# An encoder trunk in fp32: where the last sums of seven-product pairs are split, the order of the down pieces, the place of the norm's bias, and when the pooling bands are loaded

## The chip, the core and the metric

One of the eight cores of a Trainium2 chip runs the whole program. The metric is the device time of one execution in microseconds (us): a median over runs, and for single traces the span from the first to the last instruction. The engines have separate instruction queues, each worked through in its own order: PE multiplies matrices (weights are loaded by its second queue, PEld), DVE and ACT work on vectors, POOL does a little, SP issues the DMA transfers. A wait is a semaphore between two of them.

## The reference

Two post-norm layers over 256 tokens of width 2048, batch 1, all in fp32:

```
x <- LN(alpha*x + mixer(x));  x <- LN(alpha*x + SwiGLU(x))
def swiglu(x, w_gate, w_up, w_down):
    return (jax.nn.silu(x @ w_gate) * (x @ w_up)) @ w_down
def layer_norm(x, g, b):
    mu = jnp.mean(xf, axis=-1, keepdims=True)
    var = jnp.mean(jnp.square(xf - mu), axis=-1, keepdims=True)
    return ((xf - mu) * lax.rsqrt(var + LN_EPS)).astype(x.dtype) * g + b
```

Layer 0's mixer is neighbourhood attention beside a gated recurrence, layer 1's is a multi-scale pooling mixer beside grouped-query attention; each has an input and an output projection. The feed-forward width is 5632.

## The kernel before

**Splitting.** Each fp32 operand is held as a sum hi + lo of two rounded fp32r tensors, and a product takes three matmuls (`mm3`: lo x hi, hi x hi, hi x lo). `split` writes hi with an ACT cast (L122) and lo with a DVE subtraction (L123). The two token tiles of 128 rows are `tok` 0 and 1.

**Weights.** `load_half` brings a 512 KB piece (256 rows by 512 columns) into a buffer `raw` (four of them, in a ring), and splits it into `whi` and `wlo`; in the feed-forward units these have four buffers too, so a cast of `whi` waits until PE is done with the piece four before it.

**The feed-forward part.** The 5632 hidden columns are eleven chunks of 512. `whole` computes chunks 0 and 1 with plain products. The other nine are `unit`s 2 to 10. A unit computes gate and up products of its chunk for both token tiles together. For five of its eight row pairs (`SEVEN`, pairs 3 to 7) it uses a scheme of seven products in place of eight: `load_seven` loads 1 MB (`rs`), forms sums of weight blocks in `z`, and splits them into `sh` and `sl` (two buffers each). The first half of a unit runs four of the seven products for each of the five pairs (12 matmuls into the four banks `un`); between the halves some sums of the banks are formed (L488 to L493); the second half runs the other three products per pair in the order `ORDER` (3, 0, 4, 5, 1, 6, 7, 2), with plain pairs 0, 1, 2 between. One of the three, into bank c21, takes the last sum of the pair, the fourth slice of `z`. `load_seven` splits that sum too, in the first half: for the first three pairs into `zh`/`zl` (three buffers), for the last two into the room of `y4h`/`y4l`. All of `load_seven` is issued 400 places ahead of its place in the program, so the first two loads of a unit are worked on in the unit before.

**Down pieces.** The down projection of finished chunks is spread over the units by the generator `down_steps`: a round of two units (`ROUNDS`) works through the 16 pieces of two chunks: for each of four column quarters n, chunk by chunk, two pieces each; one `yield` (a step) per piece, 12 matmuls into two banks `acc`. With `run(1)` a unit runs three steps at its start, steps four to six between its first loads, and two more after the fifth load. Between steps 1, 2 and 3 stand the two `flips`: PE transposes the gated products of the previous unit, and ACT and DVE split them into that chunk's `yTh` and `yTl`. When a column quarter's last piece is done, both its banks are copied to `res` by ACT (L551), or in the first two quarters of the first round added to `res` by DVE (L549); ACT seeds a bank with `res` (L535). Unit 10 has a round of its own, with one chunk.

**Norms.** `norm` takes a token tile's statistics, subtracts the mean and multiplies by gamma on DVE (`centre`, L334), then scales by rstd on ACT (L348). `flip`, run in the middle of the next matmul chunk, transposes 512 columns at a time and adds the bias beta there, per partition from `betT`, in four ACT and four DVE instructions of 128 columns (L377, L379); `res` itself gets its beta by a DVE add (L381, L383). After the output projections that add is deferred by way of `idle_work`. There are three inner norms; the last one, which writes the output, has a branch of its own.

**Bands.** `cd_constants` loads what layer 1's mixer needs, and the banded matrices of the pooling (`band`, 1 MB, by way of two `raw` buffers), after the first of five input chunks.

The order of instructions on each engine is fixed when the program is built, by a scheduler that weighs priorities and a timing model; a row that ends `_3802` below names a tile by its number.

Of the kernel before, what the change touches and what calls it, by code (L numbers as in the profile page):

```python
# [78 lines left out]
def trunk(ctx: ExitStack, tc: tile.TileContext, a, out):  # L79
# [64 lines left out]

    idle_work = []

    def load_half(src, between=()):
# [38 lines left out]
    def mm_chunk(halves, lhs, outs, tok_major=False, after=None, before=None, seeded=False):  # L186
# [19 lines left out]
        if tok_major:  # L206
            for i, half in enumerate(halves):
                src = half[0]
                if pending and i >= FREE:
                    held[0] = 1  # L210
                loaded.append(load_half(src))
            for tok in range(NT):
                for i in range(n):
                    if pending and i >= FIRST_STEP:
                        step()
                    mms(i, tok, True)
                    if pending and tok == 0:
                        held[0] = HELD
                while pending:
                    step()  # L220
                if after:
                    after(tok)
        else:
            for i, half in enumerate(halves):
                src = half[0]
                loaded.append(load_half(src, before(i) if before else ()))
                if i >= n // 2:
                    with tc.issue_after(low[-1]):
                        for work in idle_work[:2]:
                            work()  # L230
                    del idle_work[:2]
# [74 lines left out]

    def residual_tools(res, gam, bet, betT, stats, defer=False):

# [14 lines left out]
        def norm(tok, xT=None, out_rows=None, late={}):  # L323
# [19 lines left out]
            if out_rows is None:  # L343
                for j in range(4):
                    dve = centre(j)
                for j in range(4):
                    r = cols(j)[0]
                    act = nc.scalar.activation(r, r, AF.Copy, scale=rstd[:, 0:1])  # L348
                ahead[:] = [dve.ins, act.ins]
                pending.append(flip(tok, xT))  # L350
            else:
                for j in (3, 0, 1):
                    tc.keep_in_program_order(centre(j))
                r, _, b = cols(3)
                nc.scalar.activation(r, r, AF.Copy, scale=rstd[:, 0:1])
                nc.gpsimd.tensor_tensor(r, r, b, op=add)
                for j in (0, 1, 2):
                    if j == 2:
                        tc.keep_in_program_order(centre(j))
                    tc.keep_in_program_order(scale(j))  # L360
                    store(j)
                store(3)

        def flip(tok, xT):
            for j in range(4):
                s = slice(j * NCH, (j + 1) * NCH)
                r = res[tok][:, s]
                with tc.high_priority(offset=1000):
                    t = mxp() if j % 2 else trp()
                    for k in range(4):  # L370
                        tc.keep_in_program_order(transpose(t[:, k * P : (k + 1) * P], r[:, k * P : (k + 1) * P], ident))
                    for part in range(2):
                        for k in range(4):
                            hi, lo = xT[0][tok][:, 4 * j + k, :], xT[1][tok][:, 4 * j + k, :]
                            tk, bk = t[:, k * P : (k + 1) * P], betT[:, 4 * j + k : 4 * j + k + 1]
                            if part == 0:
                                act = nc.scalar.activation(hi, tk, AF.Identity, bias=bk)  # L377
                            else:
                                dve = nc.vector.scalar_tensor_tensor(lo, tk, bk, hi.bitcast(F32), op0=add, op1=sub)  # L379
# [10 lines left out]
    def load_gb(pool, i, which):  # L390
# [3 lines left out]
        nc.sync.dma_start(b, a[f"ln_{which}_b"][i : i + 1, :].to_broadcast([P, D]))  # L394
        bT = pool.tile([P, 64], F32, tag="betT", name="betT", bufs=1)[:, :KT]
        nc.sync.dma_start(bT, a[f"ln_{which}_bT"][i])
        return g, b, bT


    def out_proj(w, order, groups, res, gb):  # L400
        seed, evac, norm = residual_tools(res, *gb, new_stats(), True)
        lhs = y_lhs(groups)
# [42 lines left out]
    def load_seven(sp, src, room):  # L445

        with tc.high_priority(offset=400):
            raw = sp.tile([P, 4, NCH], F32, tag="rs", name="rs", bufs=2)
            hi = sp.tile([P, 4, NCH], F32R, tag="sh", name="sh", bufs=2)
            lo = sp.tile([P, 4, NCH], F32R, tag="sl", name="sl", bufs=2)  # L450
            zh, zl = room or (sp.tile([P, NCH], F32R, tag=n, name=n, bufs=3) for n in ("zh", "zl"))
            z = sp.tile([P, 4, NCH], F32, tag="z", name="z", bufs=1)
            last_load[0] = nc.sync.dma_start(raw, src).ins
            nc.scalar.copy(hi[:, 0], raw[:, 0])  # L454
            nc.vector.tensor_tensor(z[:, :2], raw[:, 0:3:2], raw[:, 3:4].to_broadcast([P, 2, NCH]), op=add)
            nc.vector.tensor_tensor(z[:, 2], z[:, 0], raw[:, 2], op=add)  # L456
# [4 lines left out]
        return lambda i: (hi[:, i, :], lo[:, i, :]), (zh, zl)  # L461

# [3 lines left out]
    def unit(sp, w, lhs, forms, y, down, flips):  # L466
# [57 lines left out]
    def down_steps(w, chunks, ys, res, start):  # L524


        lhs = y_lhs(ys)
        for n in range(4):
            outs = [acc() for _ in range(NT)]
            r = [res[tok][:, n * NCH : (n + 1) * NCH] for tok in range(NT)]  # L530
            fresh = start and n < 2
            if not fresh:
                with tc.high_priority(offset=400):
                    for tok in range(NT):
                        nc.scalar.activation(outs[tok], r[tok], AF.Copy, scale=ALPHA if start else 1.0)  # L535
            steps = [(c, ci, i) for ci, c in enumerate(chunks) for i in range(2)]
            for c, ci, i in steps:
                hi, lo = load_half(w[n, 2 * c + i])
                for tok in range(NT):
                    for kk in range(2):  # L540
                        begin = (c, i, kk) == (chunks[0], 0, 0)
                        end = (c, i, kk) == (chunks[-1], 1, 1)
                        x = lhs(tok, 4 * ci + 2 * i + kk)
                        mm3(outs[tok], x, (hi[:, kk, :], lo[:, kk, :]), fresh and begin, end, True, skip_group_check=not fresh)
                half_done()
                if (c, i) == (chunks[-1], 1):
                    for tok in range(NT):
                        if fresh:
                            nc.vector.scalar_tensor_tensor(r[tok], r[tok], ALPHA, outs[tok], op0=mult, op1=add)  # L549
                        else:  # L550
                            nc.scalar.copy(r[tok], outs[tok])  # L551
                yield

    def ffn(layer, xT, res, mix_pool, close_mix, keep, last):
# [72 lines left out]
        stats = new_stats()  # L627
        seed, evac, _ = residual_tools(res, None, None, None, stats)
        yl = y_lhs([groups[c] for c in LAST])
# [325 lines left out]
    def cd_constants(pool):  # L955
# [11 lines left out]
        rcount = pool.tile([P, 4, 2, EDGE], F32, name="rcount", bufs=1)  # L967
        nc.sync.dma_start(rcount, a["rcount"])
        band = pool.tile([P, 4, NT, T], F32R, name="band", bufs=1)
        for g in range(0, 4, 2):  # L970
# [3 lines left out]
            nc.scalar.copy(band[:, s], raw)  # L974
        return cc, sn, nw, pscale, rcount, band

    def cd_mixer(mp, consts, xT, yT):
# [102 lines left out]
        for c, (kind, _) in enumerate(cd_plan()):  # L1080
            outs = [acc() for _ in range(NT)]
            mm_chunk([(a["cd_in"][c, n], two(2 * n)) for n in range(8)], lhs, outs, tok_major=(c == 0))
            if c == 0:
                with tc.issue_after(last_load[0]):
                    cc, sn, nw, pscale, rcount, band = cd_constants(consts.pop())
            if kind == "kv":
# [117 lines left out]
def layout(i):  # L1204
# [22 lines left out]
        "ln_ffn_b": f["ln_ffn_b"],  # L1227
        "ln_mix_bT": f["ln_mix_b"].reshape(2, KT, P).transpose(0, 2, 1),
        "ln_ffn_bT": f["ln_ffn_b"].reshape(2, KT, P).transpose(0, 2, 1),
    }  # L1230
# [26 lines left out]
```

## Time and profile before

| | us |
|---|---|
| median of 3 runs | 2205.69 (2205.14 to 2206.42) |
| the profiled execution | 2206.51 |
| its span | 2204.4 |
| PE busy | 2155.6 |
| DVE busy | 1704.3 |
| ACT busy | 1223.4 |
| idle time of PE ended by waits that the trace names | 37.9 |

The span is what the trace covers; the execution's own time is 2.1 us longer. The mean granted clock of PE over the span is 0.996. Matmuls of 512 columns start 0.227 us apart in steady work, so 12 of them take 2.72 us.

### The profile page before, as it was taken

How to read it: one execution, taken by the hardware profiler on the slowest of the kernel's cores; microseconds unless marked ns; L12 is line 12 of the kernel's file. 1: busy time of each engine (PE TensorE's matmuls, PEld its weight loads, DVE VectorE, ACT ScalarE, POOL GpSimd, SP SyncE). 2: the span in 40 equal slices, each digit the busy share in tenths (PEclk: the TensorE clock that was granted, in tenths of full speed). 3: DMA queues.
4: the chain of work that ended last, by engine and by line, in shares of the span. 5: the costliest groups of instructions: out<-in, count | busy, mean ns of one | idle time of the engine just before them, and what ended most of it. 6: DMA issues, size and time to landing. Idle time of an engine off the chain costs nothing. (4 is left out here: it accounts for less than half of the span.)

```text
span 2204.4 us, 27147 instructions
## 1 busy us (share of the span) xinstructions
PE 2155.6 (98%) x9910; PEld 1780.2 (81%) x9910; DVE 1704.3 (77%) x2194; ACT 1223.4 (55%) x1652; POOL 36.8 (2%) x43
## 2 busy tenths in 40 slices
PE   9999999999989999999999999999999999999998
PEld 7888888888878787887887788888787887888876
DVE  6886688667688888888886875666988888888866
ACT  6445544546455665665565654454555666566653
POOL 0000000000000000000000000000000000000000
PEclk9999999999999999999999999999999999999999
DMA  8555535674666776666665653655766666676744
GB/s 293 165 163 172 173 125 190 216 271 143 211 212 226 242 245 238 236 232 223 235 229 192 236 200 120 214 173 184 259 235 239 243 229 224 231 248 239 243 168 172
DMA packets 119190, 467.86 MB, mean 212 GB/s; under 512 B 14480, under 2 KB 17552, under 8 KB 106256
## 3 DMA queue, kind: packets, MB, share of 16 engines
q1 hardware_dynamic: 119056, 466.12, 61.7%
q8 instruction: 78, 1.28, 0.2%
q14 instruction: 56, 0.46, 0.1%
HBM read 463.97 MB, written 2.10 MB: 211 GB/s over the span
## 5 line engine op out<-in xcount | busy, mean ns | idle before, releaser
L123 DVE TENSOR_TENSOR wlo<-raw,whi 128x1024 fp32r<-128x1024 f32 (+1 forms) x671 | 815.9, 1223 | 319.1 <-ACT whi L122 312.6
L122 ACT CAST whi<-raw 128x1024 fp32r<-128x1024 f32 (+1 forms) x671 | 701.9, 1050 | 626.2 <-PE acc L296 338.6
L296 PE MATMUL acc<-whi,yTl 128*128 128x512 f32 x832 | 330.4, 397 | 13.1 <-DVE yTl L123 12.9
L296 PE MATMUL acc<-whi,yTh 128*128 128x512 f32 x832 | 325.4, 391 | 0.0
L296 PE MATMUL acc<-wlo,yTh 128*128 128x512 f32 x832 | 324.7, 391 | 0.0
L296 PE MATMUL acc<-whi,xTl 128*128 128x512 f32 x800 | 318.6, 398 | 4.9 <-ACT whi L122 4.9
L296 PE MATMUL acc<-whi,xTh 128*128 128x512 f32 x800 | 315.3, 394 | 0.0
L296 PE MATMUL acc<-wlo,xTh 128*128 128x512 f32 x800 | 313.2, 394 | 0.0
L296 PE MATMUL un<-whi,xTl 128*128 128x512 f32 x522 | 203.2, 389 | 0.0
L296 PE MATMUL un<-whi,xTh 128*128 128x512 f32 x522 | 203.1, 389 | 0.0
L296 PE MATMUL un<-wlo,xTh 128*128 128x512 f32 x522 | 203.1, 389 | 0.0
L296 PEld LDWEIGHTS acc<-whi,yTl 128*128 128x128 f32 x832 | 157.1, 189 | 48.5 <-DVE yTl L123 16.5
L296 PEld LDWEIGHTS acc<-wlo,yTh 128*128 128x128 f32 x832 | 156.9, 189 | 33.4
L296 PEld LDWEIGHTS acc<-whi,yTh 128*128 128x128 f32 x832 | 157.3, 189 | 31.3
L296 PEld LDWEIGHTS acc<-whi,xTl 128*128 128x128 f32 x800 | 151.3, 189 | 35.1 <-ACT whi L122 6.1
L296 PEld LDWEIGHTS acc<-wlo,xTh 128*128 128x128 f32 x800 | 151.1, 189 | 31.1 <-DVE wlo L123 0.6
L296 PEld LDWEIGHTS acc<-whi,xTh 128*128 128x128 f32 x800 | 151.4, 189 | 28.7
L123 DVE TENSOR_TENSOR sl<-z,sh 128x1536 fp32r<-128x1536 f32 x90 | 157.9, 1754 | 19.4 <-ACT sh L122 19.3
L122 ACT CAST sh<-z 128x1536 fp32r<-128x1536 f32 x90 | 133.0, 1478 | 16.8 <-DVE z L456 16.7
L454 ACT CAST sh<-rs 128x512 fp32r<-128x512 f32 x90 | 56.1, 624 | 149.5 <-DMA rs<-in_gu 64.7
L296 PEld LDWEIGHTS un<-wlo,xTh 128*128 128x128 f32 x522 | 98.0, 188 | 20.5
L296 PEld LDWEIGHTS un<-whi,xTh 128*128 128x128 f32 x522 | 98.0, 188 | 20.5
(279 smaller groups left out, 3093.1 us busy)
## 6 DMA issues: line engine op xcount, KB each, us to landing
raw<-in_gu SPq DMA_DIRECT2D x262, 512.0 KB, 4.4
rs<-in_gu SPq DMA_DIRECT2D x90, 1024.0 KB, 6.7
raw<-in_down SPq DMA_DIRECT2D x176, 512.0 KB, 4.4
raw<-in_ab_in SPq DMA_DIRECT2D x127, 512.0 KB, 4.2
raw<-in_cd_in SPq DMA_DIRECT2D x40, 512.0 KB, 4.2
raw<-in_ab_out SPq DMA_DIRECT2D x32, 512.0 KB, 4.5
raw<-in_cd_out SPq DMA_DIRECT2D x32, 512.0 KB, 4.3
bias<-in_na_bias SPq DMA_DIRECT2D x32, 64.0 KB, 4.0
```

The costliest lines, as they stand in the source:

```text
L122: nc.scalar.copy(hi, src)
L123: return nc.vector.tensor_tensor(lo, src, hi.bitcast(F32), op=sub).ins
L296: ins = nc.tensor.matmul(o, lhs[a], rhs[b], start=start and n == 0, stop=stop and n == 2, **more)
L454: nc.scalar.copy(hi[:, 0], raw[:, 0])
```

## The change

- `load_seven` no longer splits the last sum. It writes it as fp32 (`ze`) into a tile of its own for the first pair and into the rooms of `y4h` (pairs 4 and 5) and `y4l` (pairs 6 and 7) for the rest. `unit` splits it where the second half uses it, into two buffers `zfh`/`zfl`, with a priority of 400.
- `down_steps` takes two column quarters at a time and goes through both for the first chunk before it takes the second chunk. All four banks `acc` are in use at once, and a quarter is evacuated after the sixth and the eighth step of eight, no longer after the fourth and the eighth. The round of one chunk keeps its order.
- `norm` adds beta on DVE to the rows before they are transposed; `flip` is then one ACT cast and one DVE subtraction of 512 columns. `betT`, its loads and `idle_work` are gone.
- The bands are loaded after the second input chunk.

```
 def load_seven(sp, src, room):
-            zh, zl = room or (sp.tile([P, NCH], F32R, tag=n, name=n, bufs=3) for n in ("zh", "zl"))
-            z = sp.tile([P, 4, NCH], F32, tag="z", name="z", bufs=1)
+            z = sp.tile([P, 3, NCH], F32, tag="z", name="z", bufs=1)
+            ze = room
...
-            nc.vector.tensor_tensor(z[:, 3], z[:, 2], raw[:, 1], op=add)
+            nc.vector.tensor_tensor(ze, z[:, 2], raw[:, 1], op=add)
             nc.vector.tensor_tensor(lo[:, 0], raw[:, 0], hi[:, 0].bitcast(F32), op=sub)
-            split(hi[:, 1:], lo[:, 1:], z[:, :3])
-            split(zh, zl, z[:, 3])
+            split(hi[:, 1:], lo[:, 1:], z)
 def unit(sp, w, lhs, forms, y, down, flips):
-            if i == 3:
-                room = [x.rearrange("p (e a) t -> p e (a t)", e=2) for x in fourth()]
-            wt, edge[p] = load_seven(sp, w[p], room and [x[:, i - 3] for x in room])
+            if i % 2:
+                room = ap_.tile([P, 4, T], F32R, tag=("y4h", "y4l")[i // 2], name="ze4", bufs=1)
+                room = room.rearrange("p (e a) t -> p e (a t)", e=2).bitcast(F32)
+            own = room[:, (i + 1) % 2] if i else sp.tile([P, NCH], F32, tag="ze", name="ze", bufs=1)
+            wt, edge[p] = load_seven(sp, w[p], own)
...
-                product("c21", forms[p]["22"], edge[p])
+                with tc.high_priority(offset=400):
+                    ends = split_tile(sp, [P, NCH], edge[p], "zf", 2)
+                product("c21", forms[p]["22"], ends)
 def down_steps(w, chunks, ys, res, start):
-        for n in range(4):
-            outs = [acc() for _ in range(NT)]
-            fresh = start and n < 2
+        step = len(chunks)
+        for first in range(0, 4, step):
+            ns = range(first, first + step)
+            outs = {n: [acc() for _ in range(NT)] for n in ns}
+            fresh = start and first == 0
...
-            steps = [(c, ci, i) for ci, c in enumerate(chunks) for i in range(2)]
-            for c, ci, i in steps:
-                hi, lo = load_half(w[n, 2 * c + i])
+            for ci, c in enumerate(chunks):
+                for n in ns:
+                    for i in range(2):
+                        hi, lo = load_half(w[n, 2 * c + i])
 def norm(tok, xT=None, out_rows=None, late={}):
                 for j in range(4):
-                    dve = centre(j)
+                    centre(j)
                 for j in range(4):
-                    r = cols(j)[0]
+                    r, _, b = cols(j)
                     act = nc.scalar.activation(r, r, AF.Copy, scale=rstd[:, 0:1])
+                    dve = nc.vector.tensor_tensor(r, r, b, op=add)
 def flip(tok, xT):
-                    for part in range(2):
-                        for k in range(4):
-                            hi, lo = xT[0][tok][:, 4 * j + k, :], xT[1][tok][:, 4 * j + k, :]
-                            tk, bk = t[:, k * P : (k + 1) * P], betT[:, 4 * j + k : 4 * j + k + 1]
-                            if part == 0:
-                                act = nc.scalar.activation(hi, tk, AF.Identity, bias=bk)
-                            else:
-                                dve = nc.vector.scalar_tensor_tensor(lo, tk, bk, hi.bitcast(F32), op0=add, op1=sub)
-                if defer:
-                    idle_work.append(lambda r=r, s=s: nc.vector.tensor_tensor(r, r, bet[:, s], op=add))
-                else:
-                    nc.vector.tensor_tensor(r, r, bet[:, s], op=add)
+                    hi, lo = (x[tok][:, 4 * j : 4 * j + 4, :] for x in xT)
+                    v = t.rearrange("p (k t) -> p k t", k=4)
+                    act = nc.scalar.copy(hi, v)
+                    dve = nc.vector.tensor_tensor(lo, v, hi.bitcast(F32), op=sub)
 def cd_mixer(mp, consts, xT, yT):
+            if c == 1:
+                with tc.issue_after(last_load[0]):
+                    band = cd_bands(consts.pop())
```

The order of instructions at three places. First ACT around the fourth and fifth load of unit 6 of layer 0, before (`sh<-rs` is the cast of a load's first slice, `sh<-z` that of its three sums, `L488` the start of the sums between the halves):

```order
L122 CAST y4h<-z 128x512
L454 CAST sh<-rs 128x512
L122 CAST whi<-raw 128x1024
L122 CAST sh<-z 128x1536
L454 CAST sh<-rs 128x512
L122 CAST y4h<-z 128x512
L488 COPY g_7525<-un 128x512
```

and in the changed program at the same place:

```order
L437 CAST sh<-rs 128x512
L541 COPY res_3802<-acc 128x512
L524 ACTIVATE acc<-res_3802 128x512
L122 CAST whi<-raw 128x1024
L541 COPY res_3803<-acc 128x512
L122 CAST sh<-z 128x1536
L524 ACTIVATE acc<-res_3803 128x512
```

The casts of `y4h` are gone from here; the two copies of a column quarter and the seeds of the next, which stood some ten rows earlier, now stand between the fifth load's casts.

Second, DVE at the same place, before (`y4l` is the low part of a last sum; `L457` forms it):

```order
L123 TENSOR_TENSOR wlo<-raw,whi 128x1024
L123 TENSOR_TENSOR y4l<-z,y4h 128x512
L458 TENSOR_TENSOR sl<-rs,sh 128x512
L455 TENSOR_TENSOR z<-rs 128x1024
L456 TENSOR_TENSOR z<-z,rs 128x512
L123 TENSOR_TENSOR wlo<-raw,whi 128x1024
L457 TENSOR_TENSOR z<-z,rs 128x512
L123 TENSOR_TENSOR sl<-z,sh 128x1536
```

and changed:

```order
L123 TENSOR_TENSOR wlo<-raw,whi 128x1024
L438 TENSOR_TENSOR z<-rs 128x1024
L441 TENSOR_TENSOR sl<-rs,sh 128x512
L439 TENSOR_TENSOR z<-z,rs 128x512
L123 TENSOR_TENSOR wlo<-raw,whi 128x1024
L440 TENSOR_TENSOR ze_7431<-z,rs 128x512
L123 TENSOR_TENSOR sl<-z,sh 128x1536
```

The low part is gone; the last four rows keep their order, with the last sum going to `ze`.

Third, DVE near the start of unit 2 of layer 0, the first of its round, where the flips of chunk 1 are split (`yTl`), before:

```order
L123 TENSOR_TENSOR zl<-z,zh 128x512
L123 TENSOR_TENSOR wlo<-raw,whi 128x1024
L455 TENSOR_TENSOR z<-rs 128x1024
L123 TENSOR_TENSOR yTl<-un,yTh 128x4x128
L456 TENSOR_TENSOR z<-z,rs 128x512
L123 TENSOR_TENSOR wlo<-raw,whi 128x1024
L123 TENSOR_TENSOR yTl<-un,yTh 128x4x128
```

and changed:

```order
L123 TENSOR_TENSOR zfl<-ze_5280,zfh 128x512
L438 TENSOR_TENSOR z<-rs 128x1024
L439 TENSOR_TENSOR z<-z,rs 128x512
L123 TENSOR_TENSOR wlo<-raw,whi 128x1024
L440 TENSOR_TENSOR ze_5280<-z,rs 128x512
L123 TENSOR_TENSOR yTl<-un,yTh 128x4x128
L123 TENSOR_TENSOR wlo<-raw,whi 128x1024
L123 TENSOR_TENSOR yTl<-un,yTh 128x4x128
```

The sums of the third load now stand ahead of the first `yTl`. PE's own order has the same shapes in the same places; steps 3 and 4 of a round read other columns of the first chunk there in place of the second chunk.

More of the change, by code (lines that the diff above doesn't have):

```diff
@@ L143, in trunk @@
     first = [True]
-    idle_work = []
     def load_half(src, between=()):
@@ L226, in mm_chunk @@
                 loaded.append(load_half(src, before(i) if before else ()))
[L227 to L231, printed above, removed]
                 for kks in ((0,), (1,)) if before and i == 0 else ((0, 1),):
@@ L305, in new_stats, with residual_tools @@
         return [sm.tile([P, 4, 6], F32, tag=f"st{t}", name=f"st{t}", bufs=1) for t in range(NT)]
-    def residual_tools(res, gam, bet, betT, stats, defer=False):
+    def residual_tools(res, gam, bet, stats):
         def seed(tok, n, psum, scale):
@@ L394, in load_gb @@
         nc.sync.dma_start(b, a[f"ln_{which}_b"][i : i + 1, :].to_broadcast([P, D]))
-        bT = pool.tile([P, 64], F32, tag="betT", name="betT", bufs=1)[:, :KT]
-        nc.sync.dma_start(bT, a[f"ln_{which}_bT"][i])
-        return g, b, bT
+        return g, b
     def out_proj(w, order, groups, res, gb):
-        seed, evac, norm = residual_tools(res, *gb, new_stats(), True)
+        seed, evac, norm = residual_tools(res, *gb, new_stats())
         lhs = y_lhs(groups)
@@ L456, in load_seven @@
             nc.vector.tensor_tensor(z[:, 2], z[:, 0], raw[:, 2], op=add)
[L457 removed]
+            nc.vector.tensor_tensor(ze, z[:, 2], raw[:, 1], op=add)
             nc.vector.tensor_tensor(lo[:, 0], raw[:, 0], hi[:, 0].bitcast(F32), op=sub)
[L459 to L461 removed]
+            split(hi[:, 1:], lo[:, 1:], z)
+        return lambda i: (hi[:, i, :], lo[:, i, :]), ze
     BEGIN = ((0, "11", "c11"), (3, "f", "c12"), (1, "e", "c22"), (2, "g", "c21"))
@@ L527, in down_steps @@
         lhs = y_lhs(ys)
-        for n in range(4):
-            outs = [acc() for _ in range(NT)]
-            r = [res[tok][:, n * NCH : (n + 1) * NCH] for tok in range(NT)]
-            fresh = start and n < 2
+        step = len(chunks)
+        for first in range(0, 4, step):
+            ns = range(first, first + step)
+            outs = {n: [acc() for _ in range(NT)] for n in ns}
+            r = {n: [res[tok][:, n * NCH : (n + 1) * NCH] for tok in range(NT)] for n in ns}
+            fresh = start and first == 0
@@ L532, in down_steps @@
             if not fresh:
                 with tc.high_priority(offset=400):
-                    for tok in range(NT):
-                        nc.scalar.activation(outs[tok], r[tok], AF.Copy, scale=ALPHA if start else 1.0)
-            steps = [(c, ci, i) for ci, c in enumerate(chunks) for i in range(2)]
-            for c, ci, i in steps:
-                hi, lo = load_half(w[n, 2 * c + i])
[L539 to L552, printed above, removed]
+                    for n in ns:
+                        for tok in range(NT):
+                            nc.scalar.activation(outs[n][tok], r[n][tok], AF.Copy, scale=ALPHA if start else 1.0)
@@ new lines, in down_steps @@
+            for ci, c in enumerate(chunks):
+                for n in ns:
+                    for i in range(2):
+                        hi, lo = load_half(w[n, 2 * c + i])
+                        for tok in range(NT):
+                            for kk in range(2):
+                                begin = (ci, i, kk) == (0, 0, 0)
+                                end = (ci, i, kk) == (step - 1, 1, 1)
+                                x = lhs(tok, 4 * ci + 2 * i + kk)
+                                mm3(outs[n][tok], x, (hi[:, kk, :], lo[:, kk, :]), fresh and begin, end, True, skip_group_check=not fresh)
+                        half_done()
+                        if (ci, i) == (step - 1, 1):
+                            for tok in range(NT):
+                                if fresh:
+                                    nc.vector.scalar_tensor_tensor(r[n][tok], r[n][tok], ALPHA, outs[n][tok], op0=mult, op1=add)
+                                else:
+                                    nc.scalar.copy(r[n][tok], outs[n][tok])
+                        yield
@@ L627, in ffn @@
         stats = new_stats()
-        seed, evac, _ = residual_tools(res, None, None, None, stats)
+        seed, evac, _ = residual_tools(res, None, None, stats)
         yl = y_lhs([groups[c] for c in LAST])
@@ L968, in cd_constants, with cd_bands @@
         nc.sync.dma_start(rcount, a["rcount"])
+        return cc, sn, nw, pscale, rcount
+    def cd_bands(pool):
         band = pool.tile([P, 4, NT, T], F32R, name="band", bufs=1)
@@ L974, in cd_constants @@
             nc.scalar.copy(band[:, s], raw)
-        return cc, sn, nw, pscale, rcount, band
+        return band
     def cd_mixer(mp, consts, xT, yT):
@@ L1084, in cd_mixer @@
                 with tc.issue_after(last_load[0]):
-                    cc, sn, nw, pscale, rcount, band = cd_constants(consts.pop())
+                    cc, sn, nw, pscale, rcount = cd_constants(consts[0])
+            if c == 1:
+                with tc.issue_after(last_load[0]):
+                    band = cd_bands(consts.pop())
             if kind == "kv":
@@ L1227, in layout @@
         "ln_ffn_b": f["ln_ffn_b"],
-        "ln_mix_bT": f["ln_mix_b"].reshape(2, KT, P).transpose(0, 2, 1),
-        "ln_ffn_bT": f["ln_ffn_b"].reshape(2, KT, P).transpose(0, 2, 1),
     }
```

## The prediction

> **What bounds the kernel now.** I read the page's busy shares first, then the waits of PE alone, then the timeline around each of those waits.
>
> ```profile
> PE 2155.6 (98%) x9910; PEld 1780.2 (81%) x9910; DVE 1704.3 (77%) x2194; ACT 1223.4 (55%) x1652; POOL 36.8 (2%) x43
> ```
> ```profile
> PE acc L296 <- DVE yTl L123: 12.9, 9, 4.2
> PE un L296 <- DVE sl L123: 11.9, 18, 1.1
> PE acc L296 <- ACT whi L122: 4.9, 1, 4.9
> PE un L296 <- ACT sh L122: 2.4, 2, 1.2
> PE tr L119 <- ACT res L348: 2.2, 1, 2.2
> PE tr L119 <- DVE g L520: 1.9, 2, 1.1
> PE un L296 <- ACT un L492: 1.0, 2, 0.8
> PE un L119 <- DVE g L578: 0.7, 1, 0.7
> ```
>
> (In the second view: who waited for whom, us in total, times, longest.) PE is busy 98% of the span, and the change leaves it the same matmuls in streams of the same length. So only PE's waits can be won: 37.9 us in all, of which the 4.9 stand at the program's start, before the first weights, and the 1.9 at the two ends of the feed-forward layers, where nothing is changed. The rest, 31.1 us, is what the change can touch. Waits also cost speed behind them:
>
> ```profile
> 613.50:618.40 4.90, 4.85 (x11) 3.81 (x12) 3.62 (x5) 0.62 (x1) 0.00 (x0) 0.50 0.57 206
> 641.50:645.70 4.20, 4.16 (x11) 3.32 (x12) 4.17 (x7) 1.33 (x2) 0.00 (x0) 0.60 0.35 142
> 1572.00:1574.00 2.00, 1.66 (x6) 1.05 (x6) 2.00 (x3) 0.00 (x0) 0.00 (x0) 1.00 0.71 244
> ```
>
> (Columns: stretch, length, busy time of PE, PEld, DVE, ACT, POOL, then granted clock.) Behind the 4.24 us wait that ends at 613.55 the clock is 0.50 for 4.90 us, which loses 4.90 x 0.50 = 2.4 us; behind the two of about 1.1 us near 641 it is 0.60 for 4.2 us, 1.7 us; behind layer 1's counterpart of the first, which ends at 1572, it is 1.00.
>
> **Down pieces by chunk.** A round's first unit runs three down steps, with the previous unit's two flips between them. Now step 3 already takes the second chunk, whose transposes were issued just before:
>
> ```profile
> 877.25 0.58 ACT L122 CAST yTh<-un 128x512 fp32r<-128x512 f32 x1
> 877.38 1.22 DVE L123 TENSOR_TENSOR wlo<-raw,whi 128x1024 fp32r<-128x1024 f32 x1 [1.37 <-ACT whi L122]
> 878.52 0.68 DVE L123 TENSOR_TENSOR yTl<-un,yTh 128x512 fp32r<-128x512 f32 x1
> 879.26 0.50 PE L296 MATMUL acc<-whi,yTl 128*128 128x512 f32 x1 [0.94 <-DVE yTl L123]
> ```
>
> ```profile
> 1968.19 2.72 PE acc L296 x12
> ```
>
> After the change steps 1 to 4 all read the first chunk, and the second is first read in step 5. Between the second flip and step 5 PE has four groups of 12 matmuls (step 3, a load's first products, step 4, the next load's), 4 x 2.72 = 10.9 us by the row of the chain above; today yTl stands 2.9 us after that flip. These waits go whole. Rounds 2 to 4 have one of 0.94 each in both layers: 6 x 0.94 = **-5.6 us**. Nothing is late next there: the whi and wlo of steps 3 and 4 stand in the queues ahead of the flips' splits, as before.
>
> Round 1 has the larger ones, and there DVE is itself behind:
>
> ```profile
> 612.81 0.68 DVE L123 TENSOR_TENSOR yTl<-un,yTh 128x512 fp32r<-128x512 f32 x1
> 613.55 0.80 PE L296 MATMUL acc<-whi,yTl 128*128 128x512 f32 x1 [4.24 <-DVE yTl L123]
> 639.73 1.76 DVE L123 TENSOR_TENSOR sl<-z,sh 128x1536 fp32r<-128x1536 f32 x1 [0.51 <-ACT sh L122]
> 641.54 0.50 PE L296 MATMUL un<-sl,fnh 128*128 128x512 f32 x1 [1.06 <-DVE sl L123]
> ```
> ```profile
> L535 ACT ACTIVATE acc<-res 128x512 f32<-128x512 f32 x72 | 43.5, 604 | 3.7 <-DVE res L549 2.6
> ```
>
> (The last row groups ACT's seeds of a bank: count, busy time, mean ns.) In layer 0 the first unit loses 0.66 + 4.24 + 2.4 (clock) + 1.18 + 1.06 = 9.5 us up to the split of its fifth load. Afterwards: the new DVE order has one more sum (0.6) ahead of the first gated product, so the flip waits 1.2 in place of 0.66; the yTl wait is gone; and the evacuation of columns 0 now stands between the fifth load's sums. From the end of step 6 ACT has whi (1.05), a seed (0.60) and sh (1.48) to do before that split (1.76): 4.9 us, with DVE's evacuation (0.68, as yTl, of the same shape), wlo (1.22) and ze (0.68) beside them. PE asks for the split 17 matmuls after step 6, 17 x 2.72/12 = 3.85 us. So a wait of 1.0 is left at best, and 2.24 as today if DVE comes as late. I take 1.8 here, where the wait of 4.24 shows how late DVE is, and 1.0 in layer 1, where it is less late. Layer 0: 9.5 - 1.2 - 1.8 = **-6.5 us**; layer 1 (of the 12.9 it has what 4.24 and the 5.6 leave, 3.1): 3.1 + 1.18 + 1.06 - 1.0 = **-4.35 us**. Bounds for the pair: 0 to -2 (DVE's backlog only takes another place, and the clock at most is won) and -14 (no wait left in either).
>
> By the Trainium skill (TensorE: Matmul & The Clock Gate, Part 1) the clock falls to half after an idle window of about 3.4 us. The row at 613.5 agrees; those at 641.5 (waits of about 1.1 us) do not. By that rule no slow stretch would be left in these units, which would be 1.7 us more than my sum.
>
> **Last sums split in the second half.** DVE and ACT each lose a 128x512 split per load (0.68 on DVE) in the half where PE waits 0.59 us for the fifth load's sl. What makes that sl late is seen around that load in unit 9 of layer 0, and then in unit 10:
>
> ```profile
> 1090.16 1.05 ACT L122 CAST whi<-raw 128x1024 fp32r<-128x1024 f32 x1 [2.09 <-PE acc L296]
> 1091.12 1.48 ACT L122 CAST sh<-z 128x1536 fp32r<-128x1536 f32 x1
> 1091.25 1.23 DVE L123 TENSOR_TENSOR wlo<-raw,whi 128x1024 fp32r<-128x1024 f32 x1 [0.39 <-ACT whi L122]
> 1092.99 1.75 DVE L123 TENSOR_TENSOR sl<-z,sh 128x1536 fp32r<-128x1536 f32 x1
> 1094.80 0.50 PE L296 MATMUL un<-sl,fnh 128*128 128x512 f32 x1 [0.59 <-DVE sl L123]
> ```
> ```profile
> 1154.19 1.05 ACT L122 CAST whi<-raw 128x1024 fp32r<-128x1024 f32 x1 [0.54 <-PE acc L296]
> 1155.15 0.57 ACT L551 COPY res<-acc 128x512 f32<-128x512 f32 x1
> 1155.63 1.48 ACT L122 CAST sh<-z 128x1536 fp32r<-128x1536 f32 x1
> 1157.14 1.76 DVE L123 TENSOR_TENSOR sl<-z,sh 128x1536 fp32r<-128x1536 f32 x1
> 1158.95 0.50 PE L296 MATMUL un<-sl,fnh 128*128 128x512 f32 x1 [0.72 <-DVE sl L123]
> ```
>
> In unit 9 the chain is: PE frees a whi buffer at the end of step 6, ACT writes whi, DVE its wlo, then the last sum z, then sl. DVE sat idle 0.39 us before that wlo. The removed y4l stood ahead of that idle time, so taking it away only lengthens the idle time; the chain starts from PE. And the changed order keeps wlo, ze, sl in that order. So I expect **nothing** won from the split that moved. Worse: by chunk, the columns' evacuation comes after step 6 and no longer after step 4, so ACT's copy res<-acc now stands between whi and sh. Unit 10 has that order today (its rounds are of one chunk): sh ends later, sl starts at once after it, and PE waits 0.72, not 0.59. Units 3 to 9 of both layers should turn from 0.59 to 0.72: 14 x 0.13 = **+1.8 us**. Unit 10 stays.
>
> In the second half stand five such splits, as many as zh/zl and y4h/y4l had in both halves together, and in the new order the first two of a unit stand already in the unit before. For the third I count DVE's ops from the end of the first half: a sl of one column (0.68), wlo (1.22), z (as wide, 1.22), two wlo (2.44), z (0.68), zfl (0.68): done 6.9 us in, while PE reads it after 9 + 24 + 9 + 6 = 48 matmuls, 10.9 us. Cost 0; PE would stall in each of 18 units if that lead of 4 us went.
>
> A small gain stands beside it:
>
> ```profile
> 844.47 0.59 ACT L492 ACTIVATE un<-g 128x512 f32<-128x512 f32 x1
> 845.12 0.50 PE L296 MATMUL un<-zh,xTl 128*128 128x512 f32 x1 [0.79 <-ACT un L492]
> ```
>
> Ahead of this negation ACT now does sh (1.48) and whi (1.05); afterwards that sh stands behind it. It comes some 1.4 us earlier, against waits of 0.79 and 0.20: **-1.0 us**.
>
> **Norms and bands.** The only norm that PE waits for is the second token tile's at the end of layer 0:
>
> ```profile
> 1245.23 1.05 ACT L974 CAST band<-braw 128x1024 fp32r<-128x1024 f32 x1 [2.87 <-DMA braw<-in_band]
> 1246.06 1.12 DVE L379 SCALAR_TENSOR_TENSOR xTl<-mx,betT,xTh 128x128 fp32r<-128x128 f32 x4
> 1247.38 0.15 DVE L245 TENSOR_SCALAR rstd<-mv 128x1 f32<-128x1 f32 x1
> 1247.46 1.41 DVE L334 SCALAR_TENSOR_TENSOR res<-res,mv,gam 128x512 f32<-128x512 f32 x2
> 1248.64 1.95 ACT L348 ACTIVATE res<-res,rstd 128x512 f32<-128x512 f32 x3 [0.78 <-POOL rstd L248]
> 1249.41 0.70 PE L119 MATMUL tr<-ident,res 128*128 128x128 f32 x4 [2.24 <-ACT res L348]
> ```
>
> Two things offset each other. Ahead of its statistics DVE has sixteen small ops of the other tile's flip, four in 1.12, so 4.5 together; afterwards four of 0.68, 2.7: 1.8 us earlier. Behind them, the first transpose will wait for four centres (two in 1.41, so 2.8) and an add (0.68), 3.5 us after rstd, where ACT's first scale now ends 1.8 us after it (three in 1.95 from 1248.64): 1.7 later. I take **0**, from -2 to +1.7. The other five flips show no wait today; the sum keeps them at 0. The bands move 1 MB behind the second chunk's sixteen pieces; PE has no wait between 1250 and 1572, and eight weight buffers lead it. Cost 0; if ACT, which waited 2.87 us for the first band today, held PE as long, +3.
>
> **The sum** against the profiled execution's own 2206.51 (span 2204.4): -5.6 - 6.5 - 4.35 + 1.8 - 1.0 + 0 = -15.65, so 2190.9. That execution lies 0.8 above the median of the runs, so on those 2190.0.
>
> **Rivals.**
> 1. *The split does free the fifth load.* If DVE's queue and not the freed buffer sets sl, units 3 to 10 lose their waits too: 15.65 + 1.8 + 14 x 0.59 + 2 x 0.72 = 27 us, 2178.5. For it: DVE is the busiest engine there. Against it: 0.39 us of idle time before wlo. 13%.
> 2. *The first units' backlog moves but does not shrink*, since DVE's work there is the same: then -5.6 - 1.0 + 1.8 and 0 to 2 of the clock, 2199.5. 15%.
> 3. *The moved splits arrive late* (the other side). zfh stands in ACT's queue among whi casts that wait for PE, with two buffers; if the lead of 4 us is eaten, PE stalls before each unit's edge products. From 15.65 / 18 = 0.87 us per unit on, the gain is gone; at 1.5 us it is 2190 + 27 = 2217. The order speaks against it. 6%.
> 4. *Nothing measurable*: norm and bands at their bad ends (+4.5) on top of rival 2, 2204. 6%.
>
> Forecast 60%: 2190, its own range 2184 to 2196. About 0.2%, 4.4 us, is what can be told from no change. **Range** 2178 to 2201: it takes in rivals 1 and 2. Faster 0.87 (forecast and rivals 1 and 2, less the tail of 2 over 2201.3), same 0.07, slower 0.06.
>
> **What would show it.** PE's wait for yTl gone from the list (12.9 to under 1): right on the chunks. Its wait for sl still there, 18 times, near 0.72 each in units 3 to 9: right on the chain from PE; under 0.2 each: rival 1. In unit 2 of layer 0 no clock of 0.50, and one wait of 1 to 2.6 before the fifth load. A new line, PE un waiting for zfl or ze: rival 3. A wait for the transposes of the norm over 3.7: my offset of the two norm terms was wrong.

## The result, and the profile after

| | before | after |
|---|---|---|
| median of the runs, us | 2206.06 (2205.14 to 2208.27) | 2189.16 (2186.24 to 2191.48) |
| profiled execution, us (span) | 2206.51 (2204.4) | 2190.12 (2187.8) |
| PE's waits after its first matmul, us (times, over 0.15) | 33.0 (35) | 23.2 (26) |
| lost to half clock before the last matmul, outside PE's waits, us | 5.9 | 3.4 |

After over before is 0.9921, with an interval of 0.9904 to 0.9938: 17 us less. The forecast was 2190, its range 2178 to 2201.

The busy shares and the waits of PE alone (who waited for whom, us, times, longest), of the changed kernel:

```profile
PE 2148.9 (98%) x9910; PEld 1778.7 (81%) x9910; DVE 1691.1 (77%) x2122; ACT 1215.7 (56%) x1580; POOL 37.5 (2%) x43
```
```profile
PE un L288 <- DVE sl L123: 14.0, 18, 1.2
PE acc L288 <- ACT whi L122: 5.1, 2, 4.8
PE tr L119 <- DVE g L506: 2.9, 2, 1.6
PE tr L119 <- DVE res L341: 2.8, 1, 2.8
PE un L288 <- DVE yTl L123: 2.2, 3, 0.8
PE acc L288 <- DVE g L568: 1.1, 1, 1.1
```

The 12.9 us of waits for yTl into acc are gone, the wait for sl is still there 18 times, and that for the negation is gone. The fifth load of unit 9 in the timeline of the changed kernel (start, length, engine, line, operation, idle time before it):

```profile
1078.95 0.68 DVE L439 TENSOR_TENSOR z<-z,rs 128x512 f32<-128x512 f32 x1
1079.08 1.03 ACT L122 CAST whi<-raw 128x1024 fp32r<-128x1024 f32 x1
1080.02 0.58 ACT L541 COPY res<-acc 128x512 f32<-128x512 f32 x1
1080.15 1.23 DVE L123 TENSOR_TENSOR wlo<-raw,whi 128x1024 fp32r<-128x1024 f32 x1 [0.52 <-ACT whi L122]
1080.49 1.48 ACT L122 CAST sh<-z 128x1536 fp32r<-128x1536 f32 x1
1081.29 0.69 DVE L440 TENSOR_TENSOR ze<-z,rs 128x512 f32<-128x512 f32 x1
1082.01 1.76 DVE L123 TENSOR_TENSOR sl<-z,sh 128x1536 fp32r<-128x1536 f32 x1
1083.82 0.50 PE L288 MATMUL un<-sl,fnh 128*128 128x512 f32 x1 [0.72 <-DVE sl L123]
```

This is the order that was forecast, and its wait: 0.72 in place of 0.59. In unit 2 of layer 0, DVE is still behind:

```profile
612.89 0.69 DVE L123 TENSOR_TENSOR yTl<-un,yTh 128x512 fp32r<-128x512 f32 x1
613.63 0.50 PE L288 MATMUL un<-sh,fml 128*128 128x512 f32 x1 [0.82 <-DVE yTl L123]
614.62 0.69 DVE L123 TENSOR_TENSOR yTl<-un,yTh 128x512 fp32r<-128x512 f32 x1
615.36 0.50 PE L288 MATMUL un<-sh,fml 128*128 128x512 f32 x1 [0.77 <-DVE yTl L123]
```

No down step reads this yTl yet. PE waits because the split reads the flip's transposes out of an un bank, and the third and fourth products of the unit's first load write into the two banks that the flips took. At the end of layer 0, the second tile's norm:

```profile
1234.05 0.25 DVE L317 BATCH_NORM_AGGREGATE mv<-st 128x2 f32<-128x24 f32 x1
1235.73 0.23 DVE L954 TENSOR_SCALAR nwq<-nwq 128x128 f32<-128x128 f32 x1 [1.43 <-DMA nwq<-in_d_q_norm]
1235.87 0.15 DVE L237 TENSOR_SCALAR rstd<-mv 128x1 f32<-128x1 f32 x1
1239.40 0.63 PE L119 MATMUL tr<-ident,res 128*128 128x128 f32 x4 [2.78 <-DVE res L341]
```

DVE reaches the norm sooner, as forecast, and then stands for 1.43 us: the scaling of the next layer's small norm weights is queued between the statistics and rstd, and its load has not landed.

### The profile page after: what moved, and what is told of

The parts are those of the page before. It is cut to its first block, busy times and chain, and to the rows that moved or that the text cites. A ratio compares the mean times of both kernels' runs of the same rounds, so it can differ in the third digit from the quotient of the medians.

```text
span 2187.8 us, 27113 instructions
## 1 busy us (share of the span) xinstructions
PE 2148.9 (98%) x9910; PEld 1778.7 (81%) x9910; DVE 1691.1 (77%) x2122; ACT 1215.7 (56%) x1580; POOL 37.5 (2%) x43
## 4 chain that ended last, share of the span: by engine, by line
PE 92%; DVE 3%; ACT 3%; DMA 1%; issue 0%; SPq 0%; ACTq 0%; DVEq 0%
PE acc L288 52%; PE un L288 30%; PE mx L288 6%; PE mx L803 1%; DVE sl L123 1%; PE tr L119 1%; ACT whi L122 1%; ACT sh L122 1%; PE un L119 1%; DVE wlo L123 1%; DMA raw<-in_cd_in 0%; ACT res L541 0%; DVE res L326 0%; DMA raw<-in_ab_in 0%; PE mx L849 0%
## 5 line engine op out<-in xcount | busy, mean ns | idle before, releaser
L288 PEld LDWEIGHTS un<-whi,xTl 128*128 128x128 f32 x522 | 98.0, 188 | 20.3
```

Of the source, the lines that this page charges most:

```text
L288: ins = nc.tensor.matmul(o, lhs[a], rhs[b], start=start and n == 0, stop=stop and n == 2, **more)
```

## Experiments

Each kernel ran beside the kernel before on the same chip; "+" and "-" us are against the median of those runs (2205.8 for the first four, 2207.0 for the others). The changed kernel is at 2189.2.

### The parts alone

**e1, chunk order alone**: the changed down_steps in the kernel before.

```
- steps = [(c, ci, i) for ci, c in enumerate(chunks) for i in range(2)]
- for c, ci, i in steps:
+ for ci, c in enumerate(chunks):
+     for n in ns:
+         for i in range(2):
```

> The kernel before, with the down pieces by chunk and nothing else of the change. If the working of the prediction holds, this part carries nearly all of it: PE's wait for yTl into the acc banks goes (12.9 us in 9 waits to none), the fifth load's wait for sl in units 3 to 9 turns from 0.59 to 0.72, and the time falls by 12 to 15 us, to 2191 to 2194. If the moved splits carry the gain, it falls by no more than 6 us, to 2200 or more. In the changed kernel the first unit of each layer still waits for yTl, there into the un banks (0.82 and 0.77, and 0.57); if that wait comes from the flips' transposes and not from the moved splits, it stands here too.

Measured: **2229.4, +23.6 us** (ratio 1.0105, 1.009 to 1.012). The waits for yTl into acc went, and a new wait for sh came, 1.18 in each of units 3 to 9, with one of 1.06 for sl behind it:

```profile
PE un L296 <- ACT sh L122: 20.6, 16, 2.0
PE un L296 <- DVE sl L123: 17.9, 18, 1.1
```
```profile
1093.59 0.68 DVE L123 TENSOR_TENSOR y4l<-z,y4h 128x512 fp32r<-128x512 f32 x1
1094.79 1.22 DVE L455 TENSOR_TENSOR z<-rs 128x1024 f32<-128x1024 f32 x1
1096.53 1.23 DVE L123 TENSOR_TENSOR wlo<-raw,whi 128x1024 fp32r<-128x1024 f32 x1 [0.52 <-ACT whi L122]
1097.67 0.68 DVE L456 TENSOR_TENSOR z<-z,rs 128x512 f32<-128x512 f32 x1
1098.68 1.47 ACT L122 CAST sh<-z 128x1536 fp32r<-128x1536 f32 x1
1100.20 0.50 PE L296 MATMUL un<-sh,fnl 128*128 128x512 f32 x1 [1.18 <-ACT sh L122]
1101.99 0.50 PE L296 MATMUL un<-sl,fnh 128*128 128x512 f32 x1 [1.06 <-DVE sl L123]
```

(First the waits, then unit 9 in the timeline of e1.) The fourth load's split y4l (0.68) stands ahead of the fifth load's sums, so the second sum (L456) comes behind the wlo of the freed buffer, and sh behind that sum: it starts 3.2 us after whi (1095.46), against 1.4 in the changed kernel. Both theories missed this. That yTl is waited for into un banks stands here too (1.36 and 0.31), so the chunk order brings that, not the moved splits.

**e2, moved splits alone**: the changed load_seven and unit in the kernel before.

```
- split(zh, zl, z[:, 3])
+ nc.vector.tensor_tensor(ze, z[:, 2], raw[:, 1], op=add)
  ...
- product("c21", forms[p]["22"], edge[p])
+ ends = split_tile(sp, [P, NCH], edge[p], "zf", 2)
+ product("c21", forms[p]["22"], ends)
```

> The kernel before, with the last sums split in the second half and nothing else of the change. If the chain of the fifth load starts from PE (freed whi buffer, whi, wlo, last sum, sl), the wait for sl stays at 0.59 in units 3 to 9 and 0.72 in unit 10, the negation's waits (0.79 and 0.20) go, and the time falls by 0 to 3 us, within what can be told. If the queue of DVE or ACT sets that wait, the split that moved (0.68 of DVE, 0.58 of ACT per load) takes it away: 18 waits of under 0.2, and the time falls by 8 to 11 us.

Measured: **2198.1, -7.7 us** (0.9964, 0.9952 to 0.9976). The fifth load of unit 9:

```profile
1082.81 1.06 ACT L122 CAST whi<-raw 128x1024 fp32r<-128x1024 f32 x1 [2.10 <-PE acc L296]
1082.82 0.69 DVE L457 TENSOR_TENSOR ze<-z,rs 128x512 f32<-128x512 f32 x1
1085.28 1.76 DVE L123 TENSOR_TENSOR sl<-z,sh 128x1536 fp32r<-128x1536 f32 x1 [0.15 <-ACT sh L122]
1087.09 0.50 PE L296 MATMUL un<-sl,fnh 128*128 128x512 f32 x1 [0.24 <-DVE sl L123]
```

With the splits gone, all three sums fit into DVE's idle time ahead of wlo, and sl waits for nothing but sh: 0.24 in place of 0.59. That is between the theories: DVE's queue was part of the wait, the whi ahead of sh the rest.

**e9, both**: the edits of e1 and e2 together, without those of norm and bands.

> The kernel before, with the down pieces by chunk and the last sums split in the second half, without the edits of norm and bands. The two alone gave +23.6 and -7.7 us; if they added up this would be some 16 us slower than before, 2222. If the split's place on DVE is what the chunk order stumbled on (with it moved, the fifth load's sums stand before the freed whi's wlo), the waits are those of the whole change (18 for sl, 0.72 in units 3 to 9, none for sh), and the time is 2187 to 2192: 14 to 19 less than before.

Measured: **2185.2, -21.8 us** (0.9903, 0.9888 to 0.9918), with 18 waits for sl (14.0 us, 0.72 to 0.73 in units 3 to 9) and none for sh. So the two don't add: +23.6 - 7.7 = +15.9 became -21.8. With the chunk order in place, the moved splits are worth 23.6 + 21.8 = 45 us. The edits of norm and bands on top of e9 make the whole change. Its interval overlaps with e9's, so together they do nothing that can be told. The norm's wait does not tell it either: in the traces without these edits it lies between 1.86 (e9) and 3.22 (e2), and the changed kernel's 2.78 is among them.

**e3 and e4, norm alone and bands alone.**

```
# e3
  act = nc.scalar.activation(r, r, AF.Copy, scale=rstd[:, 0:1])
+ dve = nc.vector.tensor_tensor(r, r, b, op=add)
  ...
- act = nc.scalar.activation(hi, tk, AF.Identity, bias=bk)
+ act = nc.scalar.copy(hi, v)
# e4
+ if c == 1:
+     with tc.issue_after(last_load[0]):
+         band = cd_bands(consts.pop())
```

> The kernel before, with beta added to the rows ahead of the flip (no transposed beta) and nothing else of the change. By the prediction the shorter flip of the first token tile (1.8 us) and the longer way from rstd to the first transpose (1.7) offset each other: the norm's wait of 2.2 at the end of layer 0 stays within 0.5, and the time within 2 us. In the changed kernel that wait was 2.78, with DVE idle for 1.43 us ahead of rstd, waiting for the small norm weights' load; if that load is what eats the shorter flip, the idle time stands here too and the wait is 2.6 to 3.

> The kernel before, with the bands loaded after the second chunk and nothing else of the change. If the load is hidden in both places, the time stays within 2 us, with no new wait of PE between 1250 and 1330, and the wait at the norm stays 2.2. If the 1 MB delayed the norm weights' load or the next chunk's pieces before, the wait at the norm falls or one of up to 3 us appears in the second chunk.

Measured: e3 **2206.7, +0.8** (1.0009, 1.0001 to 1.0017), e4 **2205.3, -0.5** (0.9998, 0.999 to 1.0007). Both times as expected, but in e3 the norm's wait was 4.70, for a reason neither theory had:

```profile
1242.87 0.15 DVE L237 TENSOR_SCALAR rstd<-mv 128x1 f32<-128x1 f32 x1
1245.95 1.04 ACT L957 CAST band<-braw 128x1024 fp32r<-128x1024 f32 x1 [7.34 <-DMA braw<-in_band]
1247.18 1.04 ACT L957 CAST band<-braw 128x1024 fp32r<-128x1024 f32 x1 [0.19 <-DMA braw<-in_band]
1248.13 2.56 ACT L340 ACTIVATE res<-res,rstd 128x512 f32<-128x512 f32 x4
1249.72 0.66 PE L119 MATMUL tr<-ident,res 128*128 128x128 f32 x2 [4.70 <-DVE res L341]
```

(The norm in e3's timeline.) rstd is ready 2.2 us before PE runs out of work (at 1245.02), where before it came 0.2 behind (1247.38 and 1247.18); and ACT stands at the bands' load ahead of its scaling. With the later bands that stop is gone, and the wait for the norm weights' load is left: 2.78 in the changed kernel. So the bands' edit takes away a loss that the norm's edit alone brings, and a gain of the pair over the 2.24 before does not show.

### What is left in the changed kernel

**e5, e6, e7: ACT's order around the fifth load's sh.** In e5 the copies go behind it, in e6 the cast of the freed whi, in e7 both.

```
# e6, e7: the second half's second piece is the one that takes the buffer freed by step 6
+ hold[:] = [last_sh[0]] if (p, n) == (ORDER[1], 0) else []
- for ins in behind:
+ for ins in hold or behind:
      order.enter_context(tc.issue_after(ins))
# e5, e7: step 6's copies are put off until the fifth load is written
- nc.scalar.copy(r[n][tok], outs[n][tok])
+ copies.append(lambda n=n, tok=tok: nc.scalar.copy(r[n][tok], outs[n][tok]))
  ...
  wt, edge[p] = load_seven(sp, w[p], own)
+ with tc.issue_after(last_sh[0]):
+     while copies and i == len(SEVEN) - 1:
+         copies.pop(0)()
```

> The changed kernel, with the two evacuation copies (res<-acc) behind the fifth load's sh on ACT, and nothing else moved: whi, sh, copies. By the chain as the trace of the changed kernel shows it (whi frees DVE's wlo, then the last sum, then sl), sh ends some 0.5 us earlier but sl still starts behind wlo and the last sum, which end where sh ended before: the wait for sl stays at 0.66 to 0.73, and the time within 3 us of the changed kernel's 2189. If the copies alone made the difference between 0.72 and less, as the prediction's +1.8 us has it, the wait falls to 0.59 or less.

> The changed kernel, with the whi that waits for step 6's buffer ordered behind the fifth load's sh on ACT (so its wlo stands behind sl on DVE); copies and seeds stay ahead of sh. That whi is read only after steps 7 and 8, so it has time. If the queue behind the freed buffer makes sl late, sh starts behind copies and seeds, 0.3 us earlier than now, and sl with it: the wait falls from 0.72 to 0.3 to 0.45 in units 3 to 9, and the time by 3 to 6 us from 2189. If DVE's own work sets sl, the wait stays at 0.7.

> The changed kernel, with both the freed whi and the evacuation copies behind the fifth load's sh on ACT. Then sh starts as soon as its sums stand (0.85 us earlier than now), and nothing but sh stands ahead of sl: the 18 waits for sl (14.0 us in all) fall to under 0.2 each, units 2 perhaps excepted, and the time to 2176 to 2180. If the wait only moves, a new one shows at step 7 (wlo), at the negation or at the second half's first pieces, and the time stays over 2184.

| | us | ratio to before (interval) | sl in units 3 to 9 | waits after the start |
|---|---|---|---|---|
| changed | 2189.2 | 0.9921 (0.9904 to 0.9938) | 0.72 to 0.73 | 23.2 |
| e5 | 2183.5 | 0.99 (0.9882 to 0.9917) | 0.60 | 18.7 |
| e6 | 2204.8 | 0.9995 (0.9984 to 1.0007) | 0.66 | 33.5 |
| e7 | 2171.8 | 0.9843 (0.9825 to 0.9861) | none | 11.8 |

e5 went against the first of its expectations and for the prediction's step: the copy between whi and sh is the 0.13 of that term. In e6 the copies and seeds moved into the room that whi left, sh did not start sooner (0.66 where I expected 0.3 to 0.45), and the negation of the between-half sums became late in each of units 3 to 9:

```profile
PE un L289 <- ACT un L478: 16.1, 14, 1.2
PE un L289 <- DVE sl L444: 10.3, 16, 0.7
```

In unit 9 the negation's sum is ready at 1096.0 and the negation starts at 1097.7: a copy, a whi, a second copy and a seed stand ahead of it on ACT.

In e7 sh starts as soon as its sums stand. Unit 9:

```profile
1072.79 1.49 ACT L444 CAST sh<-z 128x1536 fp32r<-128x1536 f32 x1 [2.67 <-DVE z L441]
1074.18 1.05 ACT L122 CAST whi<-raw 128x1024 fp32r<-128x1024 f32 x1
1074.31 1.76 DVE L445 TENSOR_TENSOR sl<-z,sh 128x1536 fp32r<-128x1536 f32 x1 [0.83 <-ACT sh L444]
1076.13 0.50 PE L290 MATMUL un<-sl,fnh 128*128 128x512 f32 x1
```

whi is cast 1.8 us later than it could be (step 6 ends at 1072.37) and nobody misses it. Of 18 waits for sl two are left (1.1 us, the units 2).

**e10 and e11: the same order without the moved splits.** e10 is e1 with e7's edits, e11 the kernel before with e6's (the diff above, in the old load_seven).

> The kernel before, with the down pieces by chunk alone (which gave 2229: a wait of 1.18 for sh and one of 1.06 for sl in units 3 to 9), and with the freed whi and the copies behind the fifth load's sh on ACT. The splits of the last sums stay in the first half. If the order behind the freed buffer is the cause (the last but one sum stands behind the whi's wlo on DVE, and sh waits for it), the wait for sh goes and that for sl falls to 0.3 to 0.8: 2190 to 2202. If the work of the splits in the first half is too much for DVE in any order, the two waits stay over 1.5 us together and the time over 2215.

> The kernel before, with nothing of the change, and the whi that waits for step 6's buffer behind the fifth load's sh on ACT. There the copies stand behind step 4, not 6, so sh starts when its sums stand: the wait of 0.59 for sl in units 3 to 9 (and 0.72 in unit 10) goes, the waits of 0.93 for yTl stay, and the time falls by 8 to 12 us to 2194 to 2198. If DVE's splits in the first half set sl, the wait stays over 0.4 and the time over 2202.

Measured: e10 **2196.9, -10.1** (0.9954, 0.9942 to 0.9967), sh no longer waited for in units 3 to 9, sl 0.62, the negation 0.35. So what made the chunk order slower than before was the order behind the freed buffer. The splits' place still costs: with that same order, e10 is at -10.1 and e7, which has them moved (and the edits of norm and bands), at -35.2. e11 **2230.8, +23.7** (1.011, 1.0095 to 1.0125): the wait for sl went as expected, and a longer one took its place, which I had not looked for. The waits, then unit 9:

```profile
PE un L297 <- ACT un L494: 25.5, 16, 1.8
```
```profile
1109.60 1.48 ACT L460 CAST sh<-z 128x1536 fp32r<-128x1536 f32 x1
1109.95 0.68 DVE L493 TENSOR_TENSOR g<-g,un 128x512 f32<-128x512 f32 x1
1112.92 0.61 ACT L494 ACTIVATE un<-g 128x512 f32<-128x512 f32 x1
```

On DVE, wlo and the fifth load's y4l now stand behind sl, ahead of the between-half sums. But the last wait is ACT's: the negation (L494) could start when its sum is done (1110.63) and starts at 1112.92. Ahead of it on ACT stand sh, a seed, a whi and a copy; in the kernel before it stands behind sh and whi alone, and the copies come after it. So it is 1.78 us late in each of units 3 to 9. How much of that DVE's delay adds and how much ACT's order, no run separates. With the splits in the first half the order of e7 stays short of room: e10 has it, and keeps waits of 0.62 for sl and 0.35 for the negation.

**e8 and e12: the norm weights.** e8 is the changed kernel with their scaling behind chunk 1's pieces, e12 has e7's edits too.

```
- nc.vector.tensor_scalar(nw["q"], nw["q"], QSCALE, None, op0=mult)
  ...
  if c == 1:
+     with tc.issue_after(low[-1]):
+         nc.vector.tensor_scalar(nw["q"], nw["q"], QSCALE, None, op0=mult)
```

> The changed kernel, with the scaling of the small norm weights (128x128) on DVE moved from ahead of the second tile's norm to behind the second chunk's pieces. If DVE's 1.43 us of idle time ahead of rstd, for that load, is what the norm waits for, its wait falls from 2.78 to 1.3 to 1.5, with the stretch of slow clock behind it (1.7 us) perhaps gone too: 1.4 to 3.1 us less than the changed kernel, 2186 to 2188. If the centring and scaling behind rstd set it, the wait stays at 2.7.

> The changed kernel, with the freed whi and the copies behind the fifth load's sh (2171.8 alone) and the scaling of the norm weights behind the second chunk's pieces (2186.6 alone, 2.6 less than the changed kernel). They touch different stages, so they should add up: 2168 to 2171, with no wait over 0.6 for sl and one of 1.3 at the norm.

Measured: e8 **2186.6** (0.9912, 0.9896 to 0.9928), the norm's wait 1.26 and no slow clock behind it, though one of 0.88 came at the first tile's transposes. e12 **2170.5** (0.9838, 0.9824 to 0.9851): the fastest, 36.5 us less than before by their medians. Its waits after the start, by total:

```profile
PE tr L119 <- DVE g L516: 2.6, 2, 1.5
PE un L290 <- DVE yTl L123: 1.6, 2, 0.8
PE tr L119 <- DVE res L343: 1.3, 1, 1.3
PE un L290 <- DVE sl L445: 1.0, 2, 0.5
```

The 1.3 us to e7 are within what those runs spread (2169.1 to 2172.9); the wait in the trace, 1.26 against 2.74, is what shows the edit. Six traces agree on the cause: PE's wait at the norm is 2.78, 2.74, 1.98 and 1.84 where DVE stands 1.4, 1.4, 0.6 and 0.5 us for that load (the changed kernel, e7, e5, e6), and 1.26 where it doesn't (e8, e12). An edit against the waits for yTl in un banks was not tried.

## Why the prediction was right in its sum, and where it was wrong

- **The path.** That only PE's waits could be won held.
- **Rounds 2 to 4, -5.6.** All six waits of 0.93 went.
- **Units 3 to 9, +1.8.** Measured 14 x (0.726 - 0.594) = +1.85, with the chain and the copy in it as forecast; e5 takes that copy away and the 0.13 with it.
- **The negation, -1.0.** 0.79 and 0.20 went.
- **Unit 2, -6.5 and -4.35: mis-sized.** Layer 0 had 7.1 us of waits and keeps 0.82 + 0.77 + 1.19 = 2.8; with the 2.4 of clock that the sum counted before and the 1.7 left behind them now, 9.5 became 4.5: -5.0. Layer 1: 5.35 became 1.06 + 0.57 + 1.21 = 2.84, -2.5. The step that failed was "the yTl wait is gone": the flips' un banks keep it, at 0.6 to 1.6 us. Two of the prediction's own signs say so: the waits for yTl total 2.2 where it asked for under 1, and unit 2 of layer 0 still has a stretch at half clock. The flip's wait of 1.2 did not come in layer 0; one of 1.06 for the gated product came in layer 1, where the sum had none. The fifth load's wait was 1.19 where the sum had 1.8, and 1.21 where it had 1.0. Against that, the second slow stretch of layer 0, at 642, which the sum left out, went too (1.7).
- **The moved splits, cost 0.** That held: no wait for zfh, zfl or ze is in the list, so the lead of 4 us was enough.
- **The norm, 0 from -2 to +1.7.** +0.54, less than that wait scatters between traces (1.86 to 3.22 without the edits). The working held up to rstd, then the load of the norm weights ate what the shorter flip had won; without that load it is 1.26 (e8), 1 us less than before.
- **The ends of the feed-forward layers, "nothing is changed".** They went from 1.9 to 2.9. The same lines show 2.7 and 3.6 in e4 and e3, where nothing near them was changed either, so I count that as spread between executions.
- **"I expect nothing won from the split that moved": wrong.** It rested on the order whi, wlo, last sum, sl, which is right for the changed kernel and for the kernel before, and I took it as given in both. Alone, the split reorders DVE and wins 7.7 us (a part of rival 1); under the chunk order it wins 45, and without it that order loses 23.6. I had given the gain to the chunk order, and cost at nothing the part that makes it possible. The sum came out because it was worked out on the order of all edits together.

The profiled executions, 2206.51 and 2190.12, are 16.4 apart: 9.8 of listed waits, 2.4 of slow clock outside those waits, and 9 x 0.27 = 2.4 from there being nine waits fewer (below). The last 1.8 I can't place.

That the total agrees to 0.8 us is in part luck. The terms as forecast make 15.65; what they brought is 5.6 + 5.0 + 2.5 - 1.85 + 1.0 - 0.5 = 11.75. Things that stand in no term made up for it: 1.7 of the second slow stretch, 2.4 of what waits cost beyond their length, and the 1.8, less 1.3 at the start and at the ends of the feed-forward layers.

## What to carry to other kernels

Work out an edit's price on the instruction order of the whole change, and don't split that price among the edits: here two that gave +23.6 and -7.7 apart gave -21.8 together. On an in-order engine, a cast that a freed buffer lets go takes its place ahead of work that is wanted sooner; look when each is read, and put the one with time behind. After each wait taken away, look at the next instruction that the moved work now stands ahead of: e11 won its wait, e6 a little of it, and both lost more at the negation.

## What was not expected of the hardware

**A listed wait costs more than its length.** From the 4000th to the 4200th matmul (860 to 907 us before) the changed kernel has 0.80 us less of waits, and takes 1.08 less. In a stream matmuls start 0.227 apart (2.72 for 12) and are listed 0.39 long; a wait is counted from that end, 0.16 late, and the first matmul behind it is listed 0.50, 0.11 more: 0.27 for each wait. Short waits are therefore dearer than the list says.

**Slow clock comes in pieces of one size.** In all fourteen traces (five have none) each stretch of low clock between the first and the last matmul is 3.41 us or twice that long, at half speed: 1.71 us lost, or twice that, where PE has work throughout. Windows of the changed kernel, then of e1 (stretch, length, busy time of PE, PEld, DVE, ACT, POOL, then granted clock):

```profile
611.50:616.00 4.50, 2.91 (x12) 1.78 (x11) 4.50 (x6) 0.86 (x1) 0.00 (x0) 1.00 0.60 217
616.00:620.00 4.00, 4.00 (x12) 3.14 (x11) 2.89 (x3) 1.99 (x2) 0.00 (x0) 0.57 0.91 240
```
```profile
704.80:708.20 3.40, 3.40 (x15) 2.82 (x16) 2.93 (x4) 0.00 (x0) 0.00 (x0) 1.00 0.45 176
771.50:775.00 3.50, 3.50 (x10) 2.73 (x9) 3.14 (x5) 0.01 (x1) 0.00 (x0) 0.51 0.21 84
```

Two waits of 0.8 suffice for one (616). And the same pair of waits in e1, 1.18 and 1.06, is followed by full clock at 704.8 and by half clock at 771.5; in units 3 to 9 six of 14 pairs are, in e11 seven of 14 waits of 1.78. What decides is where a wait falls on a grid of time. In the nine traces that have such stretches, the starts of a trace's stretches lie whole multiples of 3.413 us apart, to 0.01 us: before at 611.60, then 9 and 187 such steps later, at 642.32 and 1249.89. I add up the listed waits within each step of that grid. Among the steps at full clock, all 25 that hold 1.80 us of waits or more are followed by half clock, none that holds under 1.58 is, and 11 of the 23 between are. So the pair in e1, 2.24 together, brings half clock where most of both falls into one step.

By the Trainium skill (TensorE: Matmul & The Clock Gate, Part 1) the gate looks at free-running windows of about 3.4 us, and the slow state is half speed. The traces agree with both (3.41 us, and a granted clock of 0.50). That a window must be idle for it the traces contradict: PE was busy 2.91 of the 4.50 us ahead of the stretch at 616. This is read from the traces; no run was made for it. The slow clock is part of why e1 and e11 lost more than their waits: e11 has 13.8 us more of waits than before and, outside them, 11.6 more of slow clock (17.5 and 5.9).
